# A list schedule's margin for matmuls fed by other engines, and seven edits beside it

## The chip, the cores and the metric

The kernel runs on one core of one Trainium2 chip. The metric is the device time of one execution in microseconds (us). Three runs of the kernel before took 1166.16, 1166.23 and 1167.39 us; the median is 1166.23 us. The trace is of one execution, taken by the hardware profiler.

## The reference

Two model blocks run one after the other on 256 tokens of 1024 features, in float32. The first block is two layers, each a mixer, a layer norm, a SwiGLU feed-forward part (2816 wide) and a second layer norm. The mixer of layer 0 joins stick-breaking attention and sparse attention over the 64 best keys of an indexer; that of layer 1 is differential attention. The second block puts 16 meta tokens ahead, and runs a gated linear recurrence (HGRN2) with short convolutions, an output product, a feed-forward part with a convolution, and RMS norms.

```python
def first_block(x, c, ...):
    mod = einsum('bd,ldm->lbm', silu(c), w_mod) + b_mod[:, None, :]
    for i in range(2):
        sh_m, sc_m, g_m, sh_f, sc_f, g_f = split(mod[i], 6)
        h = x * (1 + sc_m) + sh_m
        y = even_mixer(h, ...) if i % 2 == 0 else odd_mixer(h, ...)
        x = layer_norm(ALPHA * x + (1 + g_m) * y, ln_mix_g[i], ln_mix_b[i])
        h = x * (1 + sc_f) + sh_f
        y = (silu(h @ w_gate[i]) * (h @ w_up[i])) @ w_down[i]
        x = layer_norm(ALPHA * x + (1 + g_f) * y, ln_ffn_g[i], ln_ffn_b[i])

def hybrid_layer(h, lb, ...):                # second block, 16 meta tokens ahead
    q, f_raw, i_in, g_out, b_gate, c_gate, x_conv, gate_a, gate_b = split(rmsnorm(h) @ w_in)
    f = lb + (1 - lb) * sigmoid(f_raw)       # S_t = diag(f_t) S_{t-1} + (1 - f_t) v_t^T
    o = hgrn2(silu(q), 1 - f, i_in, log(f))  # o_t = S_t^T q_t
    ...
    h = h + merged @ w_out
    return h + (silu(conv(a)) * val) @ w_down   # a, val = rmsnorm(h) @ w_up
```

## The kernel before

Features lie on the partitions and the 256 tokens along the free dimension. Nearly all the work is products of activations with weights that stream from memory once, about 230 MB. A slab of weights (`stage`) is split by `fetch_half` into a high part `whi` (a copy on ScalarE) and a low part `wlo` (a subtraction on VectorE), and `mm3` multiplies the parts of weights and activations in three products per tile. The first slabs of the first product are used whole, as float32. The modulation vectors are a second stream: `mod_chunks` brings 96 chunks of 128x1024 through three buffers `mst`, and one VectorE operation multiplies and sums each.

A layer norm (`Norm`) takes its input by eight chunks `d0` to `d7` in `add`: a VectorE operation makes d from a product's bank, ScalarE squares it, and GpSimd adds the chunks into the sums `s1` and the squares into `s2`. At the last chunk, matmuls against a matrix of 1/1024 (`inv1024`) give mean and variance per token; `s1` and `s2` hold seven chunks and the eighth is a matmul operand of its own. Meanwhile the next product has started on the unnormalised operand `U`, which `scale_split` makes; these products are what TensorE can do while the statistics come. The five norms before the last are named here LN1 (after the output product of layer 0), LN2 (after its feed-forward part), LN3 and LN4 (the same in layer 1), and the RMS norm.

`gen_hgrn` runs twice, for four heads each. It first sums the log decays of the meta tokens backwards: 14 additions on GpSimd, each of which reads the one before. Then it builds a decay-weighted score matrix by levels `lv` of halved blocks: eight float32 matmuls of 128 by 128 columns into two banks, and a masked copy from each bank into `At`.

What runs when is not written out by hand. `Plan` records the operations of all engines, and `Plan.order` is a list schedule: it keeps an estimated time of each engine, and always issues the operation with the smallest due time among those that are ready. An operation becomes ready when the estimated end of what it needs, plus a gap, has come: `SELF` on one engine, `HOP` (300 ns) between two. `cost` gives the estimated duration by engine and size. Each engine then runs its list strictly in that order and waits on semaphores where something is late. Every instruction is issued from one helper, so in the profile all carry its line, L428 (L427 for ScalarE's table loads). Names in the profile are those of pools: `pa` is a PSUM bank, `w` a working tile, `sm` a small one, `cst` the constants.

Of the kernel before, what the change touches and what calls it, by code (L numbers as in the profile page):

```python
# [18 lines left out]
S = 256  # L19
# [7 lines left out]
EPS = 1e-6  # L27
# [42 lines left out]
class View:  # L70
    """A view of a planned tile; it becomes an access pattern once the tile has its buffer."""
# [33 lines left out]
class Plan:  # L105
    """Records engine operations in program order, orders them by a list schedule over estimated
    times that respects data dependences and buffer counts, and issues them in that order."""

    HOP = 300.0
    SETS = {AF.Exp: "natural_log_exp_and_others", AF.Ln: "natural_log_exp_and_others", AF.Silu: "silu_and_others",  # L110
# [67 lines left out]
    def cost(self, eng, op, writes, reads):  # L178
# [21 lines left out]
        if eng == "POOL":  # L200
            return 100.0 + n * 2.2
# [52 lines left out]
    def order(self):  # L254
# [177 lines left out]
def kernel(ctx, tc, io, out):  # L432
# [46 lines left out]
    class Vec8:  # L479
        """Feature chunks of up to 272 tokens, four to a tile."""  # L480
# [18 lines left out]
    def C(name, w=128):  # L499
        return cst[:, _C[name]:_C[name] + w]  # L500
# [66 lines left out]
    def add_plan(name, n, whole=0):  # L567
        """whole: so many slabs stay float32, and their products take float32's own passes"""
# [85 lines left out]
    def group(X, toks, ks=ALLK, outer=False):  # L654
        """one bank per column chunk; outer: the chunks advance together over k"""
# [8 lines left out]
    def gemm_pair(X):  # L664
        """both column chunks of a slab in one bank, 256 tokens"""
# [7 lines left out]
    def gemm_down(X, evac):  # L673
        """K = 2816"""
# [12 lines left out]
    def scale_split(Xh, Xl, src, g):  # L687
        """src * g in two parts, g per feature"""
# [6 lines left out]
    def root(dst, eps, src=None):  # L695
        """dst = 1 / sqrt(src + eps)"""
# [5 lines left out]
    class Norm:  # L702
        """t = ALPHA * x + (1 + g) * y by chunks, its mean and variance per token, and t * gain with
        (-gain, offset) columns as the moving operand of products that start before the statistics"""

        def __init__(self, xa, g1, lv, d=None, sq=None):
            self.xa, self.g1, self.lv, self.sq = xa, g1, lv, sq
# [8 lines left out]
        def add(self, k, y):  # L716
# [44 lines left out]
        def add_sq(self, k, d):  # L761
            """with LN = g * (t - mean) / std + b: the sums of (g t)^2, 2 g^2 t and 2 g b t"""
# [1079 lines left out]
```

## Time and profile before

| | |
|---|---|
| median of three runs | 1166.23 us |
| span of the profiled execution | 1163.9 us |
| mean granted TensorE clock | 0.989 of full speed |
| busy: TensorE, VectorE, ScalarE, GpSimd | 97%, 78%, 62%, 10% |
| read from memory | 229.8 MB, 198 GB/s over the span |

The span runs from the first to the last instruction of one execution; 2.3 us of the median run lie outside of it. PE is TensorE, DVE VectorE, ACT ScalarE, POOL GpSimd, SP the queue that issues the transfers. Since PE's ends are modelled, "97% busy" overstates it a little, and the small gaps are read from the wait rows and from the number of instructions in a stretch.

### The profile page before, as it was taken

Reading aid. Unit: us, or ns where it says so; the run is one execution under the profiler, and the core shown is the slowest. Engines: PE = TensorE matmul, PEld = TensorE weight load, DVE = VectorE, ACT = ScalarE, POOL = GpSimd, SP = SyncE. Lnnn points to the kernel's source line nnn. Section 1 sums busy time; section 2 is a strip of 40 time slices with the busy share of each in tenths; the row PEclk is TensorE's granted clock in tenths of the full one; section 3 lists DMA queues with packets and bytes.
Section 4 is the critical chain, followed back from the end, with each engine's and each line's share of the span. In section 5 each row is a group of like instructions: output and inputs, shape, how many; then the busy total and the mean of one; then the engine's idle time right before and its main releaser. Section 6 shows DMA issues by size and latency. Waiting matters only on the chain.

```text
span 1163.9 us, 22101 instructions
## 1 busy us (share of the span) xinstructions
PE 1125.9 (97%) x8769; PEld 1077.6 (93%) x8769; DVE 912.5 (78%) x1676; ACT 726.0 (62%) x1316; POOL 118.2 (10%) x127
## 2 busy tenths in 40 slices
PE   5999989999999999999999999999999999999997
PEld 4885889999999779899999999999999999999996
DVE  6799889988999999885558896896659978866642
ACT  3558657545448987664445567786758766655541
POOL 0110220000231302200003402000010011000011
PEclk9999989999999999899999999999999999999999
DMA  9938647998985425365544625244433325555441
GB/s 352 410 131 309 236 163 279 350 328 301 339 327 193 143 104 194 140 246 189 181 171 178 232 88 182 86 169 154 172 110 145 144 100 193 200 188 189 168 163 37
DMA packets 42248, 232.29 MB, mean 200 GB/s; under 512 B 4640, under 2 KB 6176, under 8 KB 24096
## 3 DMA queue, kind: packets, MB, share of 16 engines
q1 hardware_dynamic: 42144, 230.87, 54.4%
q8 instruction: 69, 1.13, 0.4%
q14 instruction: 35, 0.29, 0.1%
HBM read 229.81 MB, written 1.05 MB: 198 GB/s over the span
## 4 chain that ended last, share of the span: by engine, by line
PE 77%; DVE 11%; ACT 4%; DMA 4%; issue 2%; POOL 2%; DVEq 0%; SPq 0%; ACTq 0%; POOLq 0%
PE pa L428 77%; DVE w L428 5%; DVE wlo L428 3%; ACT w L428 2%; DMA mst<-in_wmod_dram 2%; POOL w L428 2%; DVE sm L428 2%; DVE mst L428 1%; ACT whi L428 1%; DMA whi<-in_w_dram 1%; DMA cst<-in_cst_dram 1%; ACT L427 0%; DMA vec<-in_vecs_dram 0%; ACT sm L428 0%; ACT scb L428 0%
## 5 line engine op out<-in xcount | busy, mean ns | idle before, releaser
L428 PE MATMUL pa<-w,whi 128*128 128x256 f32 (+4 forms) x5104 | 919.4, 288 | 8.5 <-DMA whi<-in_w_dram 7.6
L428 PEld LDWEIGHTS pa<-w,whi 128*128 128x128 f32 x5104 | 769.7, 190 | 16.9 <-ACT w L428 6.3
L428 PE MATMUL pa<-w,wlo 128*128 128x256 f32 (+3 forms) x2608 | 661.5, 289 | 0.0
L428 ACT ACTIVATE whi<-stage 128x1024 fp32r<-128x1024 f32 (+1 forms) x330 | 339.5, 1041 | 247.7 <-PE pa L428 217.8
L428 DVE TENSOR_TENSOR wlo<-stage,whi 128x1024 fp32r<-128x1024 f32 (+1 forms) x330 | 404.1, 1234 | 100.3 <-ACT whi L428 94.0
L428 PEld LDWEIGHTS pa<-w,wlo 128*128 128x128 f32 x2608 | 465.5, 190 | 7.0 <-issue 3.9
L428 ACT ACTIVATE w<-w 128x256 fp32r<-128x256 f32 (+9 forms) x257 | 117.3, 470 | 80.6 <-DVE w L428 66.9
L428 POOL TENSOR_TENSOR w<-w,w 128x256 f32<-128x256 f32 (+2 forms) x93 | 84.1, 917 | 521.6 <-ACT w L428 291.2
L428 ACT ACTIVATE w<-pa 128x256 f32<-128x256 f32 (+12 forms) x298 | 108.0, 392 | 46.0 <-PE pa L428 41.7
L428 DVE TENSOR_TENSOR w<-w,w 128x256 fp32r<-128x256 f32 (+7 forms) x263 | 121.5, 480 | 19.2 <-ACT w L428 15.7
L428 DVE SCALAR_TENSOR_TENSOR mst<-mst,scb 128x1024 f32<-128x1024 f32 x90 | 109.3, 1226 | 11.8 <-DMA mst<-in_wmod_dram 11.8
L428 DVE TENSOR_TENSOR w<-w,pa 128x256 f32<-128x256 f32 (+2 forms) x146 | 58.9, 418 | 60.9 <-PE pa L428 51.1
L427 ACT ACT_TABLE_LOAD x63 | 80.8, 1283 | 1.8 <-PEq L1832 0.7
L428 PE MATMUL pa<-w,w 128*128 128x128 f32 (+8 forms) x340 | 71.6, 336 | 1.2 <-DVE w L428 0.9
L428 PEld LDWEIGHTS pa<-w,w 128*128 128x128 f32 (+4 forms) x340 | 42.8, 176 | 10.6 <-issue 2.8
L428 PE MATMUL pa<-cst,w 128*128 128x128 f32 (+4 forms) x218 | 38.8, 268 | 12.6 <-POOL w L428 6.3
L428 PEld LDWEIGHTS pa<-cst,w 128*128 128x128 f32 (+2 forms) x218 | 27.8, 167 | 22.1 <-issue 7.5
L428 POOL TENSOR_TENSOR w<-w 128x256 f32<-128x256 f32 x4 | 3.2, 801 | 392.3 <-DVE w L428 392.3
L428 PE MATMUL pa<-w 128*128 128x128 f32 x240 | 35.0, 275 | 0.2 <-DVE w L428 0.2
L428 PE MATMUL pa<-whi,w 128*128 128x512 f32 x96 | 32.9, 417 | 0.0
L428 PEld LDWEIGHTS pa<-w 128*128 128x128 f32 x240 | 31.4, 191 | 0.4 <-issue 0.4
L428 POOL TENSOR_TENSOR w<-w,sinT 128x512 f32<-128x512 f32 (+1 forms) x14 | 20.4, 1454 | 107.0 <-ACT w L428 82.3
(145 smaller groups left out, 541.3 us busy)
## 6 DMA issues: line engine op xcount, KB each, us to landing
mst<-in_wmod_dram SPq DMA_DIRECT2D x90, 512.0 KB, 5.5
stage<-in_wgu_dram SPq DMA_DIRECT2D x44, 1024.0 KB, 5.0
stage<-in_wi_dram SPq DMA_DIRECT2D x36, 1024.0 KB, 4.8
stage<-in_wup_dram SPq DMA_DIRECT2D x22, 1024.0 KB, 4.8
stage<-in_wd_dram SPq DMA_DIRECT2D x24, 896.0 KB, 4.5
stage<-in_w_dram SPq DMA_DIRECT2D x15, 1024.0 KB, 7.1
stage<-in_wo_dram SPq DMA_DIRECT2D x12, 1024.0 KB, 4.8
stage<-in_wd_dram SPq DMA_DIRECT2D x12, 1024.0 KB, 4.8
```

The lines of the kernel that those rows point to most:

```text
L427: self.nc.scalar.preload_act_table_set(tables[i])
L428: fn(*[real(a) for a in args], **{k: real(a) for k, a in kw.items()})
```

## The change

Eight edits are made together.

- The schedule takes a TensorE operation as ready 1300 ns, not 300 ns, after the end of an operation on another engine that it needs (`SAFE`).
- The estimate for GpSimd rises from 100 + 2.2 n to 260 + 2.45 n ns.
- `inv1024` is no longer loaded but set on GpSimd. The first loads bring fewer columns of the constants and the vectors, the rest follows after the first product's loop, and the rotary tables are made at k = 5, not at k = 1.
- The mean of x is accumulated inside that loop, two chunks at a time, not behind it.
- LN2 and LN4 fold the eighth chunk into `s1` and `s2` with two VectorE additions; the statistics then take 4 matmuls, not 8.
- In both attentions of layer 0 the products with V, which fill 64 of the array's 128 columns, are written in pairs of the two halves.
- The decay sum of the meta tokens is done by doubling: four VectorE additions on 128 elements in place of 14 on GpSimd.
- At levels below 7 the decay matmuls move only the 64 columns that the mask keeps, into one bank, and one masked copy of half the size follows in place of two.

```diff
+    SAFE = 1000.0
...
         if eng == "POOL":
-            return 100.0 + n * 2.2
+            return 260.0 + n * 2.45
...
-                    at[j] = max(at[j], end + (self.SELF[e] if oj[0] == e else self.HOP))
+                    at[j] = max(at[j], end + (self.SELF[e] if oj[0] == e else self.HOP + self.SAFE if oj[0] == "PE"
+                                              else self.HOP))
...
-    run.sync.dma_start(vec, io["vecs"])
+    run.sync.dma_start(vec[:, :104], io["vecs"][:, :104])
     cst = const("cst", NCST)
-    run.sync.dma_start(cst[:, :128], io["cst"][:, :128])
+    run.sync.dma_start(cst[:, :130], io["cst"][:, :130])
+    inv1024 = const("inv1024", 128)
+    G.memset(inv1024, 1.0 / 1024)
...
             if k == 7:
                 sums = [(self.s1, d), (self.s2, sq)]
+                if self.fold:
+                    V.tensor_add(self.s1, self.s1, d)
+                    V.tensor_add(self.s2, self.s2, sq)
+                    sums = [(self.s1,), (self.s2,)]
...
-        if k == 1:
-            run.sync.dma_start(cst[:, 128:], io["cst"][:, 128:])
...
-        if k == 1:
+        if k % 2:
+            for kk in (k - 1, k):
+                T.matmul(ps_x, C("inv1024"), x0[kk // 4][:, kk % 4, :], start=kk == 0, stop=kk == 7)
+        if k == 5:
             rope_tables()
+    run.sync.dma_start(vec[:, 104:], io["vecs"][:, 104:])
+    run.sync.dma_start(cst[:, 130:], io["cst"][:, 130:])
...
-            for a in range(2):
-                for st in range(t + 1):
+            for st in range(t + 1):
+                for a in range(2):
                     T.matmul(ps[a * 64:a * 64 + 64, :].rearrange("p (j q) -> p j q", j=4), vtok[:, st, 0:64],
...
-        V.tensor_copy(su[:, 14, 0, :], lfm[:, :, 15])
-        V.memset(su[:, 14, 1, :], 0.0)
-        for s in range(13, -1, -1):
-            G.tensor_add(su[:, s], su[:, s + 1], lfm[:, None, :, s + 1].to_broadcast([128, 2, 4]))
+        su = su[:, 0:16]
...
+        for d in (1, 2, 4, 8):
+            V.tensor_add(sv[:, 0:16], su[:, 0:16], su[:, d:16 + d])
+            su, sv = sv, su
...
-                for hp in range(2):
-                    ps = bank("ps_h")
-                    for a in range(2):
-                        for t in range(2):
-                            xs = Xt[:, 2 * hp + a, t * 128:t * 128 + 128]
-                            T.matmul(ps[:, (a * 2 + t) * 128:(a * 2 + t) * 128 + 128], xs, xs, start=True, stop=True,
-                                     skip_group_check=True)
+                ps = bank("ps_h").rearrange("p (q i b) -> p q i b", q=8, b=B)
+                for h in range(4):
+                    for t in range(2):
+                        xs = Xt[:, h, t * 128:t * 128 + 128]
+                        T.matmul(ps[:, 2 * h + t], xs, xs.rearrange("p (i c b) -> p c i b", c=2, b=B)[:, 1], start=True,
+                                 stop=True, skip_group_check=True)
```

The order of every engine changes with the two edits of the schedule. The first place is VectorE ahead of LN1. Before, one modulation chunk (`mst`) stands between the norm's vectors (`lnv0lmg`) and d0 to d3 (`w_3_1286`, made from four banks):

```order
L428 TENSOR_TENSOR w_1_1270<-lnv0lmg_133,w_14_1266 128x4x2
L428 SCALAR_TENSOR_TENSOR mst_1216,raw_185<-mst_1216,scb_169 128x1024
L428 SCALAR_TENSOR_TENSOR w_3_1286<-pa_1099,mod_193,w_8_382 128x256
L428 SCALAR_TENSOR_TENSOR w_3_1286<-pa_1103,mod_193,w_8_382 128x256
L428 SCALAR_TENSOR_TENSOR w_3_1286<-pa_1120,mod_193,w_8_382 128x256
L428 SCALAR_TENSOR_TENSOR w_3_1286<-pa_1144,mod_193,w_8_382 128x256
L428 TENSOR_TENSOR wlo_1316<-stage_896,whi_1275 128x1024
```

Now four of these chunks stand there (one of them just ahead of the first row shown), and the low part of the last stick-breaking output (`w_18_1061`) between them:

```order
L430 TENSOR_TENSOR w_1_1265<-lnv0lmg_403,w_5_1261 128x4x2
L430 SCALAR_TENSOR_TENSOR mst_1208,raw_165<-mst_1208,scb_158 128x1024
L430 SCALAR_TENSOR_TENSOR mst_1233,raw_165<-mst_1233,scb_158 128x1024
L430 TENSOR_TENSOR w_18_1061<-pa_1273,w_4_1056 128x256
L430 SCALAR_TENSOR_TENSOR mst_1256,raw_165<-mst_1256,scb_158 128x1024
L430 SCALAR_TENSOR_TENSOR w_3_1320<-pa_1077,mod_173,w_8_355 128x256
L430 SCALAR_TENSOR_TENSOR w_3_1320<-pa_1096,mod_173,w_8_355 128x256
```

Three chunks have moved ahead of d0, and with it ahead of all that follows on VectorE.

The second place is VectorE at LN3, between d0 to d3 and d4 to d6 (`w_4_5431`). Before, two weight splits (`wlo`) and the operands U of all of d0 to d3 stand ahead of d4:

```order
L428 SCALAR_TENSOR_TENSOR w_18_5259<-w_15_5322,lnv1lmg_157,w_12_5254 128x256 x3
L428 TENSOR_TENSOR wlo_5393<-stage_5029,whi_5317 128x1024
L428 SCALAR_TENSOR_TENSOR w_18_5259<-w_15_5322,lnv1lmg_157,w_12_5254 128x256
L428 TENSOR_TENSOR wlo_5415<-stage_5188,whi_5386 128x1024
L428 SCALAR_TENSOR_TENSOR w_4_5431<-pa_5231,mod_193,w_3_3616 128x256
L428 SCALAR_TENSOR_TENSOR w_4_5431<-pa_5346,mod_193,w_3_3616 128x256
L428 SCALAR_TENSOR_TENSOR w_4_5431<-pa_5391,mod_193,w_3_3616 128x256
```

Now d4 (`w_4_5371`) stands ahead of both splits, and the others come one by one:

```order
L430 SCALAR_TENSOR_TENSOR w_18_5254<-w_0_5305,lnv1lmg_411,w_12_5250 128x256 x3
L430 SCALAR_TENSOR_TENSOR w_4_5371<-pa_5235,mod_173,w_3_3614 128x256
L430 TENSOR_TENSOR wlo_5379<-stage_5072,whi_5361 128x1024
L430 SCALAR_TENSOR_TENSOR w_18_5254<-w_0_5305,lnv1lmg_411,w_12_5250 128x256
L430 TENSOR_TENSOR wlo_5406<-stage_5121,whi_5382 128x1024
L430 SCALAR_TENSOR_TENSOR w_4_5371<-pa_5346,mod_173,w_3_3614 128x256
```

Here d4 has moved up by two weight splits and one U operation.

The third place is the decay sum of the meta tokens in the first half of `gen_hgrn`. Before, VectorE only prepares it (the copy and the memsets of `w_10_8450`), the 14 additions run on GpSimd, and VectorE takes their result for the decayed key `w_6_8515` behind three weight splits:

```order
L428 COPY w_10_8450<-w_2_8279 128x4
L428 MEMSET w_10_8450 128x4 x2
L428 TENSOR_TENSOR wlo_8456<-stage_8156,whi_8433 128x1024
L428 TENSOR_TENSOR wlo_8476<-stage_8314,whi_8447 128x1024
L428 MEMSET w_10_8450 128x4
L428 SCALAR_TENSOR_TENSOR w_4_8443<-w_7_8428,vec_98,w_4_8443 128x258 x2
L428 MEMSET w_6_8515 128x256
L428 MEMSET w_3_8521 32x128
L428 TENSOR_TENSOR wlo_8525<-stage_8314,whi_8466 128x1024
L428 TENSOR_TENSOR w_6_8515<-w_10_8450,w_2_8279 128x4x16 x2
```

Now all of it stands on VectorE, with the convolution's operations (`w_1_8450`, 258 columns) between; the decayed key is `w_10_8496`:

```order
L430 COPY w_7_8455<-w_2_8254 128x14x4
L430 TENSOR_TENSOR w_6_8463<-w_7_8455 128x128
L430 TENSOR_TENSOR w_7_8455<-w_6_8463 128x128
L430 SCALAR_TENSOR_TENSOR w_1_8450<-w_9_8426,vec_101,w_1_8450 128x258
L430 TENSOR_TENSOR w_6_8463<-w_7_8455 128x128
L430 TENSOR_TENSOR w_7_8455<-w_6_8463 128x128
L430 MEMSET w_7_8455 128x4
L430 SCALAR_TENSOR_TENSOR w_1_8450<-w_9_8426,vec_101,w_1_8450 128x258
L430 MEMSET w_10_8496 128x256
L430 TENSOR_TENSOR w_10_8496<-w_7_8455,w_2_8254 128x4x16 x2
```

The chain has moved from GpSimd to VectorE, and no weight split stands within it.

## Rows read from the trace of the kernel before

**Rows 1.** The page: busy time by engine, and the chain that ended last

```profile
PE 1125.9 (97%) x8769; PEld 1077.6 (93%) x8769; DVE 912.5 (78%) x1676; ACT 726.0 (62%) x1316; POOL 118.2 (10%) x127
PE 77%; DVE 11%; ACT 4%; DMA 4%; issue 2%; POOL 2%; DVEq 0%; SPq 0%; ACTq 0%; POOLq 0%
```

**Rows 2.** TensorE's waits: releaser, us in total, times, longest us

```profile
PE pa L428 <- DMA whi<-in_w_dram: 7.6, 3, 4.8
PE pa L428 <- DVE w L428: 6.4, 10, 2.1
PE pa L428 <- POOL w L428: 6.3, 4, 3.0
```

**Rows 3.** Stretches: length, then PE, PEld, DVE, ACT, POOL busy, PEclk, DMA, GB/s

```profile
200.00:220.00 20.00, 20.00 (x172) 20.00 (x171) 18.30 (x31) 12.94 (x18) 0.00 (x0) 1.00 0.93 346
155.00:161.80 6.80, 6.80 (x33) 6.80 (x34) 4.75 (x12) 2.11 (x3) 0.00 (x0) 0.50 0.74 265
472.40:479.30 6.90, 6.53 (x30) 6.54 (x31) 4.90 (x10) 1.82 (x3) 0.31 (x1) 0.51 0.49 161
721.60:728.40 6.80, 6.80 (x32) 6.54 (x32) 5.60 (x9) 5.00 (x7) 0.00 (x0) 0.50 0.44 154
```

**Rows 4.** Timeline of TensorE at the start: start, us, [idle before, releaser]

```profile
17.24 2.07 PE L428 MATMUL pa<-w,cst 128*128 128x256 f32 x4 [2.19 <-DMA cst<-in_cst_dram]
```

**Rows 5.** Timeline at LN1, all engines; last, transfers 130 to 145 us, issue to landing

```profile
153.20 0.38 PE L428 MATMUL pa<-cst,w 128*128 128x1 f32 x2 [2.98 <-POOL w L428]
137.66 1.66 DVE L428 SCALAR_TENSOR_TENSOR w<-pa,mod,w 128x256 f32<-128x256 f32 x4
149.96 0.47 DVE L428 SCALAR_TENSOR_TENSOR w<-pa,mod,w 128x256 f32<-128x256 f32 x1
158.67 1.22 DVE L428 SCALAR_TENSOR_TENSOR mst<-mst,scb 128x1024 f32<-128x1024 f32 x1
132.21 5.89 SPq L428 DMA_DIRECT2D mst<-in_wmod_dram  x4
mst<-in_wmod_dram SPq DMA_DIRECT2D x4, 512.0 KB, 4.5
```

**Rows 6.** The stretch of layer 1's attention, columns as in Rows 3

```profile
371.00:456.00 85.00, 80.69 (x522) 68.00 (x521) 82.52 (x195) 73.37 (x200) 15.36 (x11) 1.00 0.41 147
```

**Rows 7.** Timeline at LN3: TensorE, VectorE, GpSimd

```profile
471.10 1.05 PE L428 MATMUL pa<-cst,w 128*128 128x1 f32 x8 [2.08 <-POOL w L428]
461.71 1.76 DVE L428 TENSOR_TENSOR wlo<-stage,whi 128x1024 fp32r<-128x1024 f32 x1
465.41 1.25 DVE L428 SCALAR_TENSOR_TENSOR w<-pa,mod,w 128x256 f32<-128x256 f32 x3
466.02 6.69 POOL L428 TENSOR_TENSOR w<-w,w 128x256 f32<-128x256 f32 x6 [1.96 <-DVE w L428]
```

**Rows 8.** Timeline at the meta tokens: first half on four engines, second on GpSimd

```profile
711.95 6.86 POOL L428 TENSOR_TENSOR w<-w,w 128x8 f32<-128x8 f32 x14 [45.06 <-ACT whi L428]
718.84 0.31 ACT L428 ACTIVATE w<-w 128x128 f32<-128x128 f32 x1 [4.05 <-POOL w L428]
719.59 0.27 PE L428 MATMUL pa<-cst,w 128*32 128x128 f32 x1 [1.48 <-DVE w L428]
850.04 5.20 POOL L428 TENSOR_TENSOR w<-w,w 128x8 f32<-128x8 f32 x14 [131.24 <-DVE w L428]
```

**Rows 9.** TensorE's float32 matmuls, timeline: LN2's statistics, a decay level

```profile
346.83 1.62 PE L428 MATMUL pa<-cst,w 128*128 128x1 f32 x14
880.07 1.95 PE L428 MATMUL pa<-w 128*128 128x128 f32 x16
```

**Rows 10.** TensorE by form: xcount, busy us, mean ns, idle before

```profile
L428 PE MATMUL pa<-w,w 128*128 128x512 f32 x36 | 18.6, 598 | 0.0
L428 PE MATMUL pa<-w,w 128*64 128x512 f32 x12 | 4.1, 613 | 0.0
L428 PE MATMUL pa<-w,w 128*64 128x256 f32 x16 | 3.3, 404 | 0.0
L428 PE MATMUL pa<-w,w 128*64 128x128 f32 x16 | 2.1, 279 | 0.0
```

More of the change, by code (lines that the diff above doesn't have):

```diff
@@ L41 @@
 _n = 0
-for _name, _w in (("ident", 128), ("tn", 128), ("neg1", 128), ("inv1024", 128),
-                  ("causal", 128), ("strict", 128), ("inv", 1), ("sgn", 1)):
+for _name, _w in (("ident", 128), ("inv", 1), ("sgn", 1), ("tn", 128), ("neg1", 128),
+                  ("causal", 128), ("strict", 128)):
     _C[_name] = _n
@@ L499, in C @@
     def C(name, w=128):
-        return cst[:, _C[name]:_C[name] + w]
+        return inv1024[:, :w] if name == "inv1024" else cst[:, _C[name]:_C[name] + w]
     def VC(name, j, w=1):
@@ L702, with __init__ @@
     class Norm:
-        def __init__(self, xa, g1, lv, d=None, sq=None):
-            self.xa, self.g1, self.lv, self.sq = xa, g1, lv, sq
+        def __init__(self, xa, g1, lv, d=None, sq=None, fold=False):
+            self.xa, self.g1, self.lv, self.sq, self.fold = xa, g1, lv, sq, fold
             self.d = d or Vec8("d", S)
@@ L903 @@
     ws, pss = [], [gbank("ps_g") for _ in range((NST + 1) // 2)]
+    ps_x = bank("ps_s")[:, :S]
     for k in range(8):
@@ L921 @@
             split(X[0][k], X[1][k], Xf[k])
-    ps = bank("ps_s")
-    for k in range(8):
-        T.matmul(ps[:, :S], C("inv1024"), x0[k // 4][:, k % 4, :], start=k == 0, stop=k == 7)
     xm = w1("xm")[:, :S]
-    A.activation(xm, ps[:, :S], AF.Copy, scale=ALPHA)
+    A.activation(xm, ps_x, AF.Copy, scale=ALPHA)
     for k in range(8):
@@ L1135, in gen_sb @@
                          start=True, stop=False, skip_group_check=True)
+            for a in range(2):
+                h = 2 * j + a
                 T.matmul(ps[a * 64:a * 64 + 64, 128:256], vsb[:, 1, h * 64:h * 64 + 64],
@@ L1207 @@
     lv = ln_vectors(0, "lfg", "lfb", MV(1, 1, 0, 8), MV(1, 0, 0, 8))
-    norm = Norm(xa, MV(0, 5, 0, 8), lv)
+    norm = Norm(xa, MV(0, 5, 0, 8), lv, fold=True)
     gemm_down(Gp, norm.add)
@@ L1359 @@
     norm = Norm(xa, MV(1, 5, 0, 8), lnh, [H[k][:, NM:] for k in range(8)],
-                (lfg, lnh[:, 32:40], lnh[:, 40:48], lnh[:, 48:51]))
+                (lfg, lnh[:, 32:40], lnh[:, 40:48], lnh[:, 48:51]), fold=True)
     for i in range(2):
@@ L1439, in gen_hgrn @@
     def gen_hgrn(half, kt, km, q, P, lfm, vt, vm, qm):
-        su = w1("su")[:, :128].rearrange("p (s c h) -> p s c h", s=16, c=2)
-        V.memset(su[:, 15, 0, :], 0.0)
+        su, sv = [w1(n)[:, :192].rearrange("p (s c h) -> p s c h", s=24, c=2) for n in ("su", "sv")]
+        V.memset(su[:, 14:24], 0.0)
+        V.memset(sv[:, 16:24], 0.0)
+        V.tensor_copy(su[:, 0:15, 0, :], lfm[:, :, 1:16].rearrange("p h s -> p s h"))
+        V.tensor_copy(su[:, 0:14, 1, :], lfm[:, :, 1:15].rearrange("p h s -> p s h"))
+        for d in (1, 2, 4, 8):
+            V.tensor_add(sv[:, 0:16], su[:, 0:16], su[:, d:16 + d])
+            su, sv = sv, su
         V.memset(su[:, 15, 1, :], -1.0e4)
-        V.tensor_copy(su[:, 14, 0, :], lfm[:, :, 15])
-        V.memset(su[:, 14, 1, :], 0.0)
-        for s in range(13, -1, -1):
-            G.tensor_add(su[:, s], su[:, s + 1], lfm[:, None, :, s + 1].to_broadcast([128, 2, 4]))
+        su = su[:, 0:16]
         A.activation(su, su, AF.Exp)
@@ L1481, in gen_hgrn, with tiles @@
         V.memset(Sx, 0.0)
+        def tiles(t):
+            return t.rearrange("p a b -> p (a b)").rearrange("p (q n) -> p q n", n=128)
         def quads(t, hp):
@@ L1756, in lay_out @@
     cst[:, _C["neg1"]:_C["neg1"] + 128] = -1.0
-    cst[:, _C["inv1024"]:_C["inv1024"] + 128] = 1.0 / 1024
     cst[:, _C["causal"]:_C["causal"] + 128] = np.where(i[None, :] <= i[:, None], 0.0, NEG)
```

7 lines of the change are left out of this document (4 added, 3 removed).

## The prediction

> **What bounds the kernel now.** I read the page first. TensorE is busy for 1125.9 of 1163.9 us and makes up 77% of the chain that ended last, VectorE 11%, GpSimd 2% [rows 1]. So the kernel is bound by TensorE almost everywhere, and a change can win in three ways: less work on TensorE, a shorter wait of TensorE, or a better granted clock. The next view is the list of what TensorE waited for [rows 2]: transfers 7.6 us (all at the start), VectorE 6.4 in ten waits, GpSimd 6.3 in four. That is small, and it is all that a schedule can give back, apart from the clock. The third view is a table of stretches [rows 3]. At full clock 20 us hold 172 matmul records, 0.116 us each. In three stretches of 6.8 to 6.9 us the granted clock is at 0.50, the lower level of 1.2 GHz; they hold 30 to 33 records where 58 to 59 would fit, so each costs some 3 us. Each comes behind a place where TensorE stood still: 2.98 us at LN1 [rows 5], 2.08 us at LN3 [rows 7], 1.48 us at the meta tokens [rows 8]. Which of these waits goes, and whether its slow stretch goes with it, is the main question.
>
> **The start.** TensorE waits 2.19 us for the constants, and only for the rotary tables' transposes [rows 4]. The change moves both behind other work and takes some 0.4 MB (734 columns of 128 rows, and the 128 of `inv1024`) from ahead of the weights that are waited for, but one modulation chunk now comes earlier in the queue. Bounds 0 and 2.2; since the start is bound by transfers anyway, I take **-0.8**.
>
> **Products with V.** 64-column matmuls take 4.1 + 3.3 + 2.1 = 9.5 us [rows 10]. One of 512 columns takes 4.1/12 = 0.34 us a record where one over the whole array takes 18.6/36 = 0.52; so the two halves overlap in part already (0.66). If pairs overlapped wholly the ratio would be 0.5, and 9.5 x (1 - 0.5/0.66) = 2.3 us would go. Bounds 0 and 2.3; **-1.5**. The Trainium skill's page "TensorEngine Tiling (Array Packing)", section "Theoretical Speedup", allows up to twice the speed at 64 columns, which would be the same upper bound; the 0.66 shows that the written order now reaches it only in part.
>
> **LN1.** Here the change adds a wait. Three more modulation chunks stand on VectorE ahead of d0 to d3. In the trace they came far later, the first at 158.67 [rows 5]. The queue issues these transfers until 132.21 + 5.89 = 138.1 us, and one lands 4.5 us after its issue [rows 5], so the last of them lands at about 142.3, and its operation takes 1.22: d0 moves from 137.66 to about 143.5. (TensorE's order agrees in direction: the last products that d0 needs come some 40 products later.) From d0 to d6 VectorE took 149.96 - 137.66 = 12.3 us [rows 5]; with one U operation more d6 comes at about 156.5. Before, GpSimd was behind: the statistics waited until 153.20, 3.2 us after d6 began. Now d4 and d5 are summed early, and one addition of about 0.9 us (6.69/6 is 1.1 [rows 7]) follows d6: the first statistics matmul comes at about 158, 4.9 us later. TensorE has 9 more products to do before it (9 x 0.116 = 1.0). What is queued behind: the weight splits on VectorE, all 5 to 6 us later, hence TensorE's products on them. Bounds: -1 if the chunks land early enough for d0 to stay, +7 if the delay of d6 counts in full; **+3.5**. The slow stretch behind LN1 stays.
>
> **Folds at LN2 and LN4.** Eight matmuls fewer, two records each; LN2's took 1.62/14 = 0.116 us a record [rows 9]: 16 x 0.116 = 1.9 us. The four VectorE additions lie beside U's products; uncovered they would cost some 0.5 us each. Bounds -1.9 and 0; **-1.5**.
>
> **Layer 1's attention.** VectorE is busy for 82.5 of 85 us, TensorE shows 522 records and 80.7 us [rows 6]. By the order VectorE has some 2.4 us less to do there (two weight splits or chunks moved out). VectorE sets the pace here, so up to 2.4 us come back, less where TensorE waits for ScalarE (73.4 us busy); **-1.5**.
>
> **LN3.** GpSimd's second half waited 1.96 us for d4 [rows 7], which began at 465.41 behind two splits, the first at 461.71. Now d4 comes before both, so GpSimd can run through from the first half, some 2 us earlier, and d5, d6 follow one by one. TensorE's wait was 2.08. Bounds -2.7 (with the second wait there) and +0.5; **-2.0**.
>
> **Meta tokens.** 14 dependent additions on GpSimd take 6.86 us; ScalarE waits 4.05 us for them, TensorE 1.48 [rows 8]. The four doublings on VectorE are of 128 elements, and stand early enough to be done before TensorE asks; the second half has the same chain (5.20) with a wait of some 0.5. Next late is ScalarE's exponential, which is no longer held up. **-2.0**, bounds -2.5 and 0.
>
> **Decay levels.** 7 levels x 8 matmuls x 2 halves = 112 matmuls, 224 records. A record of 128 columns takes 1.95/16 = 0.122 us, one of a single column 1.62/14 = 0.116 [rows 9]. So columns hardly matter, and halving them gives at most 224 x 0.006/2 = 0.7; I take **0**. The smaller masked copies relieve VectorE where TensorE is the bound: 0. The Trainium skill speaks otherwise, in "TensorE: Matmul & The Clock Gate", section "Back-to-back issue gap": 134 cycles for 128 columns and about 60 for up to 64, which at 2.4 GHz would be 31 ns a record, 6.9 us in all. The row with one column speaks against it: whatever sets that record's time, it is not its columns.
>
> **The margin elsewhere.** A later ready time puts other products ahead of one that depends on another engine. What it saves is bounded by the remaining VectorE waits, some 3 us; what it can cost (a chain that goes back and forth moves on later) I bound by the same 3. **0**.
>
> **Clock.** One slow stretch of about 3 us goes, at LN3 or at the meta tokens, where the wait ahead of it goes: **-3.0**, bounds 0 and -6.
>
> **Sum.** -0.8 - 1.5 + 3.5 - 1.5 - 1.5 - 2.0 - 2.0 - 3.0 = -8.8. The span becomes 1155.1; with 2.3 us that lie around it in the median run, **1157.4 us**.
>
> **The rivals.** *Both slow stretches go and LN1 costs nothing:* 8.8 + 3 + 3.5 = 15.3 less, 1151 us. For it: the chunks' buffers may come free earlier; against it: 142.3 is read straight from the queue. *Hidden:* only fold, V and meta tokens count, LN1 costs its 3.5 and the clock stays: 1.5 + 1.5 + 2 - 3.5 = 1.5 less, 1164.7 us. For it: TensorE is 97% busy, and work freed on VectorE in layer 1 may only meet ScalarE. *Slower:* d0 waits for its three chunks, and all the splits behind it are late as well; TensorE runs dry inside the second group of the output product and again at d6 and d7: 7 us, and a longer standstill keeps the lower clock for a second stretch of 3 us. With only fold, V and meta tokens gained (5), that is 5 us more, 1171 us. It decides once LN1 costs over 7 us, which is when the last chunk lands after some 144 us. For it: VectorE is the engine that is late there. *Narrowing pays:* if half the columns took half the time, 224 x 0.122/2 = 13.7 us would go on top, 1144 us; with rows 9 against it, little chance.
>
> **How the numbers follow.** Forecast (own range 1153 to 1163.5) 0.47, both stretches 0.15, narrowing 0.04, hidden 0.16, slower 0.18. A measurement of this kernel tells 0.2%, 2.3 us, from no change. Faster: 0.47 + 0.15 + 0.04 = 0.66; same 0.16; slower 0.18. The range leaves out narrowing, the far part of the first rival and the far half of the slower one: 1149 to 1169.
>
> **What would show it.** Right: the wait for GpSimd at LN3 under 0.5 us; no wait ahead of the decayed key's transposes; at LN1 d0 near 143.5, with a wait of TensorE of 5 us or more in all; a record of 64 columns at a decay level as long as one of 128; at most two stretches at 0.50 after the start. Wrong: LN1 with no longer wait than 3 us, three slow stretches or none, or a lower mean time of a record at the decay levels. New waits in the list of TensorE's waits of over 3 us in total, on VectorE, would show that the margin costs.

## The result: 1.2% slower

The changed kernel took 1178.77 to 1187.27 us, median 1180.02, against 1166.2 for the kernel before: a ratio of 1.0118, 95% interval [1.0088, 1.0148]. The forecast was 1157.4, the range ended at 1169. The profiled execution has a span of 1176.8 us where it was 1163.9. The first rows of its page, and TensorE's waits (releaser, us in total, times, longest us), to be held against [rows 1, 2]:

```profile
span 1176.8 us, 22069 instructions
PE 1128.3 (96%) x8753; PEld 1077.6 (92%) x8753; DVE 912.1 (78%) x1676; ACT 718.1 (61%) x1309; POOL 108.4 (9%) x100
PE 76%; DVE 15%; ACT 4%; DMA 2%; issue 2%; SPq 0%; POOL 0%; DVEq 0%; ACTq 0%; POOLq 0%
```

```profile
PE pa L430 <- DVE w L430: 10.2, 11, 3.1
PE pa L430 <- DMA w<-in_xT_dram: 8.4, 2, 5.1
PE pa L430 <- ACT w L430: 6.6, 10, 1.4
PE pa L430 <- DVE wlo L430: 3.9, 6, 1.9
PE pa L430 <- DMA cst<-in_cst_dram: 3.4, 1, 3.4
PE pa L430 <- POOL w L430: 1.4, 2, 1.1
```

The work is the same and VectorE's share of the chain has grown from 11 to 15%. GpSimd, which held up TensorE for 6.3 us, now does so for 1.4; VectorE, with its weight splits, does so for 14.1 where it was 6.4.

**Where the time went.** Both kernels run the same 7856 products with streamed weights, nearly in the same order. So I took the start of the n-th of them in both traces and looked at how the lag grows from stage to stage. The stages are cut at products 420 (139 us of before), 700, 2080, 2300 (372 us), 2900, 4300, 4740, 4780 (731 us), 6000 (921 us) and 6100. Changes of the lag to the kernel before, in us, one profiled execution each:

| run | to LN1 | LN1 | LN2 | layer 1's attention, LN3 | LN4 to the meta tokens | meta tokens | decay levels | recurrence's end | all |
|---|---|---|---|---|---|---|---|---|---|
| the change | 2.9 | 5.1 | 6.3 | -1.7 | 2.4 | -6.0 | -0.7 | 5.3 | 12.6 |
| e1: no margin | 2.8 | -0.4 | -0.4 | 3.5 | -0.7 | -4.4 | 4.5 | -4.0 | 0.5 |
| e2: nor GpSimd estimate | 0.9 | 1.4 | -0.4 | 3.8 | 4.0 | -7.2 | 4.4 | -4.0 | 2.3 |
| e3: before, margin | 5.4 | 5.8 | 4.5 | -3.8 | 0.8 | -3.7 | -1.8 | 0.2 | 7.0 |
| e4: before, GpSimd estimate | 0.1 | 1.6 | 5.0 | -2.5 | 0.7 | -1.9 | 0.8 | 0.2 | 3.8 |
| e5: margin not at the norms | 2.9 | 8.1 | 4.4 | -3.1 | 3.9 | -6.0 | -0.7 | 8.2 | 17.0 |
| e6: nor in the recurrence | 2.3 | 8.1 | 4.4 | -1.5 | 2.3 | -7.3 | 4.3 | -4.6 | 7.9 |
| e7: no folds | 1.8 | 5.1 | 5.6 | -0.8 | 2.4 | -6.0 | -0.6 | 7.6 | 13.8 |
| e9: margin on products only | 4.8 | -3.5 | 6.1 | -5.2 | 5.0 | -7.2 | 4.3 | -4.0 | -0.4 |
| e10: on the small ones only | 5.8 | 3.0 | 1.6 | 1.1 | 1.0 | -4.8 | -0.6 | 8.8 | 14.3 |
| e8: before, decay sum and V | 0.8 | 0.1 | 0.0 | 0.0 | 0.2 | -3.1 | 0.5 | 0.0 | -1.4 |
| e11: e8 and levels | 2.4 | 0.2 | 0.0 | -0.6 | 2.8 | -4.4 | 4.2 | -4.0 | -0.6 |
| e12: e11 and folds | -0.3 | 0.1 | 6.6 | -1.6 | 1.3 | -2.9 | 5.8 | -4.0 | 3.8 |
| e13: margin of 300 ns | 1.2 | -2.1 | 7.6 | -6.2 | 1.7 | -2.9 | 3.8 | -4.6 | -1.4 |
| e14: e8, margin of -300 ns | 3.7 | 1.7 | 0.0 | 1.2 | 5.1 | -7.5 | -0.8 | 0.2 | 4.3 |

(The feed-forward stages and the end, where nothing moved by over 1.6 us, are left out of the columns but not of the sum. To the recurrence's levels and its end belong one another's gains and losses: a step that moves from one into the other shows in both.)

Three things have to be kept in mind with this table.

- An entry is one execution. e8 and e11 have the same order on TensorE up to some 700 us, as have e5 and e6, and their entries up to there still differ by up to 2.6 us. Executions of one kernel differ with the granted clock: e8's twelve take from 1159.58 us at a mean clock of 0.991 to 1166.06 us at 0.986. And e3's traced execution took 1172.82 us where its other three took 1178.58 to 1180.14.
- LN2 has to be read with the stage behind it. All nine runs that lose 4 us or more at LN2 gain in that stage, 0.8 to 6.2 us; in the change 6.3 - 1.7 = 4.6 us are left.
- The levels have to be read with the recurrence's end. There the change loses -0.7 + 5.3 = 4.6 us, e1 4.5 - 4.0 = 0.5.

The change loses at three places: 2.9 + 5.1 = 8.0 us up to the end of LN1, then at LN2 and at the recurrence's end.

**LN1** on VectorE and TensorE in the change (start, us, [idle before, releaser]); the last row is of the kernel before:

```profile
144.09 1.22 DVE L430 SCALAR_TENSOR_TENSOR mst<-mst,scb 128x1024 f32<-128x1024 f32 x1
146.07 1.66 DVE L430 SCALAR_TENSOR_TENSOR w<-pa,mod,w 128x256 f32<-128x256 f32 x4 [0.76 <-PE pa L430]
159.23 0.47 DVE L430 SCALAR_TENSOR_TENSOR w<-pa,mod,w 128x256 f32<-128x256 f32 x1
120.90 0.58 PE L430 MATMUL pa<-w,whi 128*128 128x256 f32 x1 [2.62 <-DVE w L430]
141.89 0.87 PE L430 MATMUL pa<-w,w 128*64 128x256 f32 x8
153.92 0.39 PE L430 MATMUL pa<-w,wlo 128*128 128x256 f32 x1 [1.90 <-DVE wlo L430]
161.47 0.38 PE L430 MATMUL pa<-inv,w 128*128 128x1 f32 x2 [1.12 <-POOL w L430]
177.43 0.47 PE L430 MATMUL pa<-w,whi 128*128 128x256 f32 x2 [0.87 <-DVE w L430]
133.63 0.88 PE L428 MATMUL pa<-w,w 128*64 128x256 f32 x8
```

Where [rows 5] had d0 at 137.66, it comes at 146.07, 8.4 us later. It stands behind the chunks, but they are not what delays it: VectorE waited for only one of them, 0.36 us, and at d0 it waits 0.76 us for TensorE's bank. Layer 0's last products with V, whose output the last products for d0 to d3 need, come 8.3 us later than before (141.89 and 133.63). In all sixteen kernels d0 follows the start of these eight by 3.1 to 5.0 us. The stage ahead already loses: at 120.90 a product waits 2.62 us for its operand (before, 0.28 us at 123.93). d6 comes at 159.23 (149.96 before), TensorE waits 1.90 us for a weight split, and the statistics start at 161.47 (153.20). Behind them are waits for h, the last of them 0.87 us, that the kernel before did not have.

**LN2** had no wait before. Now TensorE reaches the products on h before h is there:

```profile
368.62 0.38 PE L430 MATMUL pa<-w,whi 128*128 128x256 f32 x1 [0.22 <-DVE w L430]
369.90 0.58 PE L430 MATMUL pa<-w,whi 128*128 128x256 f32 x1 [0.78 <-ACT w L430]
371.15 0.77 PE L430 MATMUL pa<-w,whi 128*128 128x256 f32 x2 [0.67 <-DVE w L430]
```

The order tells why. Behind the broadcast transposes 61 products on U stood before, which took 7.3 us; in the change 26 stand there, and 38 instead of 27 between the last statistic and the transposes. The products that were to cover the chain from the transposes to h had been spent ahead of it. (In the runs below TensorE waits for h here by more than 0.3 us only where 26 or 30 products are left, in the change and in e10. The other losses at LN2 come with waits for weight splits, see the folds.)

**The recurrence's end** shows the same. The last decay level (128x128) stands behind all products that were left, 14.7 us after the level before it (6.7 us in the kernel before), and then nothing is left to cover the chain that follows: 1.36 + 0.69 + 3.06 us of waits.

```profile
921.97 1.90 PE L430 MATMUL pa<-w 128*128 128x64 f32 x16
936.69 1.16 PE L430 MATMUL pa<-w 128*128 128x128 f32 x8 [1.36 <-ACT w L430]
938.54 3.05 PE L430 MATMUL pa<-w,w 32*32 32x128 f32 x24 [0.69 <-ACT w L430]
944.64 0.51 PE L430 MATMUL pa<-w,whi 128*128 128x258 f32 x2 [3.06 <-DVE w L430]
```

**The clock.** Stretches as in [rows 3], six of the change at the lower level and one at the meta tokens:

```profile
14.90:25.20 10.30, 5.73 (x14) 4.53 (x15) 5.56 (x11) 1.09 (x2) 0.00 (x0) 0.50 1.03 408
120.70:124.10 3.40, 3.20 (x6) 1.99 (x7) 2.41 (x4) 0.03 (x1) 0.00 (x0) 0.50 0.70 248
154.90:158.30 3.40, 3.40 (x19) 3.40 (x18) 3.40 (x4) 1.39 (x2) 2.99 (x3) 0.50 0.82 296
178.80:182.20 3.40, 3.40 (x18) 3.40 (x17) 3.35 (x8) 3.37 (x7) 0.00 (x0) 0.50 0.02 5
369.90:376.70 6.80, 6.13 (x27) 5.86 (x28) 6.80 (x17) 6.65 (x13) 0.00 (x0) 0.50 0.00 0
486.00:492.80 6.80, 6.80 (x33) 6.80 (x33) 4.11 (x10) 3.27 (x4) 0.00 (x0) 0.50 0.71 252
723.00:730.00 7.00, 7.00 (x61) 7.00 (x60) 6.42 (x20) 5.85 (x11) 0.00 (x0) 1.00 0.40 150
```

At the meta tokens it stays at full speed, 61 records in 7 us where 32 were in 6.8. In exchange there is a slow stretch behind LN2's waits (27 records in 6.8 us, so some 31 fewer than fit, 3.6 us), and one of 3.4 us behind the wait at 120.90. Between the start, where TensorE waits for transfers, and the last 10 us the kernel before has 20.5 us in three stretches at the lower level, the change 23.8 us in five. So in sum the clock gave nothing back: its mean is 0.982 where it was 0.989.

### The profile page after: what moved, and what is told of

It is laid out like the page before. It is cut to its first block, busy times and chain, and to the rows that moved or that the text cites. A ratio compares the mean times of both kernels' runs of the same rounds, so it can differ in the third digit from the quotient of the medians.

```text
span 1176.8 us, 22069 instructions
## 1 busy us (share of the span) xinstructions
PE 1128.3 (96%) x8753; PEld 1077.6 (92%) x8753; DVE 912.1 (78%) x1676; ACT 718.1 (61%) x1309; POOL 108.4 (9%) x100
## 4 chain that ended last, share of the span: by engine, by line
PE 76%; DVE 15%; ACT 4%; DMA 2%; issue 2%; SPq 0%; POOL 0%; DVEq 0%; ACTq 0%; POOLq 0%
PE pa L430 76%; DVE w L430 8%; DVE wlo L430 4%; ACT w L430 3%; DVE sm L430 2%; DMA w<-in_xT_dram 1%; DVE mst L430 1%; ACT whi L430 1%; DMA mst<-in_wmod_dram 0%; DVE lbt L430 0%; SPq L430 0%; POOL w L430 0%; ACT L429 0%; DVE lnh L430 0%; DVEq L1855 0%
## 5 line engine op out<-in xcount | busy, mean ns | idle before, releaser
L430 ACT ACTIVATE w<-w 128x256 fp32r<-128x256 f32 (+8 forms) x257 | 116.9, 468 | 78.7 <-DVE w L430 66.0
L430 DVE TENSOR_TENSOR w<-w,w 128x256 fp32r<-128x256 f32 (+6 forms) x267 | 123.7, 482 | 10.0 <-ACT w L430 7.9
L430 POOL TENSOR_TENSOR w<-w,w 128x256 f32<-128x256 f32 (+1 forms) x65 | 75.4, 1182 | 528.0 <-ACT w L430 477.7
L430 PE MATMUL pa<-w,w 128*128 128x128 f32 (+8 forms) x340 | 65.5, 330 | 3.5 <-DVE w L430 1.2
L430 PEld LDWEIGHTS pa<-w,w 128*128 128x128 f32 (+4 forms) x340 | 39.9, 172 | 12.3 <-ACT w L430 3.4
L430 PE MATMUL pa<-w 128*128 128x64 f32 (+1 forms) x240 | 29.5, 270 | 1.4 <-ACT w L430 1.4
L430 PEld LDWEIGHTS pa<-w 128*128 128x128 f32 x240 | 28.8, 191 | 1.6 <-ACT w L430 1.6
L430 DVE SCALAR_TENSOR_TENSOR w<-pa,vec,w 128x256 f32<-128x256 f32 (+1 forms) x48 | 23.1, 481 | 5.7 <-PE pa L430 5.0
L430 PE MATMUL pa<-cst,w 128*128 128x128 f32 (+2 forms) x122 | 25.2, 274 | 2.2 <-DVE sm L430 1.2
```

Of the source, the lines that this page charges most:

```text
L430: fn(*[real(a) for a in args], **{k: real(a) for k, a in kw.items()})
```

## The experiments

Ratios are to the kernel before on the same chip.

**The margin alone.** e1 sets it to 0 in the change; e2 takes the GpSimd estimate back as well; e3 and e4 put the one or the other into the kernel before.

```diff
-    SAFE = 1000.0
+    SAFE = 0.0        # e1, e2
-            return 260.0 + n * 2.45
+            return 100.0 + n * 2.2    # e2
```

> The changed kernel with the margin SAFE set to 0, all else kept. Theory M (the margin): it makes the schedule put products on U ahead of the statistics' transposes (38 between the last statistic and the transposes at LN2 where 27 stood), so only 26 products on U are left behind them (61 before) and TensorE runs dry; here 46 stand behind them at LN2 and 56 at LN1. M expects the losses at LN1 (6.9 us), behind LN2 (5 to 7) and at the end of the second half of the recurrence (5.7) to go, and the gains at the meta tokens (5.9) to stay: 1156 to 1163 us. Theory E (the other edits moved the order, the margin is innocent): 1176 to 1182 us. Theory S (any edit scatters the list schedule by some us either way): anywhere from 1160 to 1180 with new losses at other places.

> The changed kernel without the margin and with the old GpSimd estimate: only the six code edits. M: 1156 to 1164, within 3 us of the run without the margin alone. E: 1176 to 1182. A theory that the GpSimd estimate does the harm at LN1 (it also sets where VectorE's modulation chunks stand ahead of d0) expects the difference between this and the run without the margin alone to be over 4 us.

> The kernel before with the margin of 1000 ns alone. M: the same loss as in the change without its gains at the meta tokens: 40 to 44 products on U are left behind the transposes at LN1 to LN3 (59, 61, 57 before), so TensorE waits for h behind LN1 and LN2 and the recurrence's end comes late: 1172 to 1185 us. E: within 3 us of before, 1163 to 1169.

> The kernel before with the higher GpSimd estimate alone. M: within 3 us of before, since 53 to 60 products on U stay behind the transposes: 1163 to 1169. The theory that the GpSimd estimate does the harm at LN1: 1170 to 1175.

Measured: e1 0.9999 [0.9980, 1.0017], 1166.95 us; e2 1.0012 [0.9995, 1.0029], 1168.53 us; e3 1.0098 [1.0062, 1.0133], 1178.97 us; e4 1.0028 [1.0010, 1.0045], 1169.8 us. The margin costs what the whole change costs, on either base: theory E falls. Theory S, that any edit scatters the schedule, does not fall by e1, whose time lies in its range. But of all runs of this section, the five kernels with 1000 ns on the small operations of attention and recurrence (the change, e3, e5, e7, e10) lie 0.9 to 1.2% above the kernel before, e6, which frees the recurrence, 0.6%, and the nine others between -0.5 and 0.3%. M was too hopeful of the rest (1156 to 1163 us for e1): without the margin the losses at LN1, LN2 and the recurrence's end are gone and the meta tokens' gain is there, yet other stages (layer 1's attention 3.5, up to LN1 2.8) give it back. And the GpSimd estimate is not quite innocent: 5.0 us at LN2. In e3 d0 at LN1 comes even later, and TensorE waits 2.65 us for GpSimd. At the recurrence's end, where M expected a loss, e3 has none: the last level stands 8.1 us behind the one before it, and no wait follows. The narrowed levels without the margin (e11) have none either, so the loss there needs the margin together with another of the edits; which one was not tried.

```profile
149.92 1.66 DVE L430 SCALAR_TENSOR_TENSOR w<-pa,mod,w 128x256 f32<-128x256 f32 x4
165.46 0.38 PE L430 MATMUL pa<-cst,w 128*128 128x1 f32 x2 [2.65 <-POOL w L430]
929.90 1.06 PE L430 MATMUL pa<-w 128*128 128x128 f32 x8
```

**Which operations' margin.** TensorE's operations have banks by their use, so the margin can be left off by bank. e5 leaves it off at the norms' statistics and transposes, e6 in the recurrence too; e9 keeps it on products with streamed weights only, e10 on all but these.

```diff
-self.HOP + self.SAFE if oj[0] == "PE"
+self.HOP + (0.0 if any(x[:4] in ("ps_s", "ps_b") for x in oj[6]) else self.SAFE) if oj[0] == "PE"          # e5
+self.HOP + (0.0 if any(x[:4] in ("ps_s", "ps_b", "ps_h") for x in oj[6]) else self.SAFE) if oj[0] == "PE"  # e6
+self.HOP + (self.SAFE if any(x[:4] in ("ps_g", "ps_d", "ps_v") for x in oj[6]) else 0.0) if oj[0] == "PE"  # e9
+self.HOP + (0.0 if any(x[:4] in ("ps_g", "ps_d", "ps_v") for x in oj[6]) else self.SAFE) if oj[0] == "PE"  # e10
```

> The changed kernel with the margin kept everywhere but at the norms' statistics and broadcast transposes (those with a bank of the statistics or of the broadcast). M, as it stands now: at each norm the margin moved these few operations behind products on U, which are then missing behind them. 40 products stand behind the transposes at LN2 here (26 in the change, 61 before), 49 at LN1 (39, 59). So the 6 us lost behind LN2 go, and some 2 to 3 of the 7 at LN1; the loss at the end of the recurrence (6) stays: 1169 to 1174 us. If LN's order is not the reason: 1178 to 1182.

> As the run with the norms freed of the margin, and free of it also in the recurrence's decay sums and scores (operations with a bank of that part). M: the last level stood 14.7 us behind the level before it since the margin put all remaining products ahead of it, and 5 us of waits followed; that goes too: 1162 to 1168 us. If the recurrence's end comes late for another reason (fewer steps per level since the levels were narrowed): as the run with the norms freed alone, within 2 us.

> The changed kernel with the margin only on products with streamed weights (operations with a bank of the products), none on the small operations of attention, norms and recurrence. Theory M2: the harm comes from chains that go back and forth between TensorE and other engines (statistics, attention, decay levels), where each TensorE step is put later; the products themselves have their operands long before. 44 to 61 products on U stay behind the transposes. So the losses behind LN2 and at the recurrence's end go and most of the one at LN1: 1164 to 1170 us. Theory M3: it is the products' own margin (on weight splits and on outputs of the attention) that makes d0 at LN1 late and lets the splits run dry behind LN2: 1173 to 1181.

> The opposite: the margin only on the small operations, none on the products with streamed weights. Only 28, 30 and 39 products on U stay behind the transposes at LN1 to LN3 (59, 61, 57 before). M2: the full loss, 1176 to 1184 us, with the last decay level 12 us or more behind the one before it. M3: 1164 to 1171.

Measured: e5 1.0106 [1.0074, 1.0138], 1180.58 us, a miss; e6 1.0056 [1.0035, 1.0078], 1174.35 us, a miss too; e9 0.9998 [0.9979, 1.0016], 1166.56 us; e10 1.0092 [1.0057, 1.0126], 1178.11 us. In total the pair e9 and e10 settles M2 against M3: the margin on the products is free, that on the small operations is the whole loss. (M2 also expected LN2's loss to go in e9, and it did not: 6.1 us, of which the stage behind it gives back 5.2.) e6 against e5 shows the recurrence: levels and end together go from 7.5 to -0.3 us, as the last level comes 6.3 us behind the one before it; in e10 it is 14.7 again, with the wait of 3.05. First e6, then e10:

```profile
918.96 1.89 PE L430 MATMUL pa<-w 128*128 128x64 f32 x16
925.22 1.05 PE L430 MATMUL pa<-w 128*128 128x128 f32 x8
```

```profile
920.52 1.89 PE L430 MATMUL pa<-w 128*128 128x64 f32 x16
935.22 1.16 PE L430 MATMUL pa<-w 128*128 128x128 f32 x8 [1.36 <-ACT w L430]
943.17 0.76 PE L430 MATMUL pa<-w,whi 128*128 128x258 f32 x2 [3.05 <-DVE w L430]
```

What fell is my reading of LN1: freeing the statistics and transposes (e5) made it worse, 8.1 us. Ahead of LN1, e6 and e9 differ only in the small operations of layer 0's attention with its indexer, and in a few transposes at the start. The last products with V begin at 141.30 us in e6 and at 138.66 in e9, and the loss up to the end of LN1 goes from 10.4 us to 1.3; e6 spends 17.1 us up to there at the lower clock, e9 6.8. So LN1's loss comes from the margin inside layer 0's attention, whose outputs the last products ahead of d0 need, and not from the statistics.

**The folds.** e7 takes them out of the change; e12, below, puts them into a kernel without margin.

```diff
-    norm = Norm(xa, MV(0, 5, 0, 8), lv, fold=True)
+    norm = Norm(xa, MV(0, 5, 0, 8), lv)
-                (lfg, lnh[:, 32:40], lnh[:, 40:48], lnh[:, 48:51]), fold=True)
+                (lfg, lnh[:, 32:40], lnh[:, 40:48], lnh[:, 48:51]))
```

> The changed kernel without the folds at LN2 and LN4. The loss behind LN2 appears with the change (6 us) but hardly with the margin alone on the kernel before (1 us), so the fold is a partner in it: two more VectorE additions ahead of the statistics, and 26 products left behind the transposes. Here 40 are left. M: 4 to 5 us of the 6 go, less 1.9 for the eight matmuls that come back: 1175 to 1179 us. If the fold is innocent: 1180 to 1183.

Measured: 1.0108 [1.0078, 1.0138], 1180.97 us, no difference to the change. The waits behind LN2 were then others (for weight splits), and the loss there was 5.6 us instead of 6.3.

**Edits without the schedule's.** e8 is the kernel before with the decay sum by doubling and the paired products with V; e11 adds the narrowed levels, e12 the folds. The edits' code is that of the change.

> The kernel before with two edits alone, the decay sum by doubling on VectorE and the paired products with V; neither moves the norms in TensorE's order (59, 61, 57 products on U behind the transposes, as before). Products with V: 64-column matmuls took 9.5 us before and 7.2 in the change, so 1 to 2.3 us. Decay sum: the change gained 6 us over that stretch, the change without the margin 4.4; 3 to 6 us with the slow stretch behind it gone, 1.5 if that stays. Together 1158 to 1163 us, and faster than both kernels. If the gains at the meta tokens came from the margin or from the whole reshuffle: 1164 to 1167.

> The kernel before with the whole edit of the recurrence (decay sum by doubling and narrowed levels with one masked copy) and the paired products with V; the order up to the recurrence is that of the run with decay sum and pairs alone (1163.0 us). Narrowing takes no time off a matmul (0.112 us a record at 64 columns as at 128), but there is one masked copy and one step fewer at each level; the change without the margin gained 5.2 us from the meta tokens to the RMS norm, the run with the decay sum alone 2.6. If that difference is due to the levels: 1159 to 1161.5 us. If it was the order: 1162 to 1165.

> As the run with the recurrence and the pairs, with the folds at LN2 and LN4 added. The folds take eight matmuls, 1.9 us, off TensorE but leave 46 products on U behind LN2's transposes (61 without). If those still cover the chain: 1 to 2 us faster than without the folds. If not (the first VectorE additions come ahead of the statistics, and the order behind moves): the same or up to 4 us slower.

Measured: e8 0.9954 [0.9936, 0.9973], 1163.01 us; e11 0.9964 [0.9942, 0.9986], 1164.51 us; e12 1.0025 [1.0010, 1.0041], 1169.86 us. e8 beats both kernels, on its two edits alone: the transposes at the meta tokens have no wait any more (1.48 us in [rows 8]),

```profile
719.63 0.27 PE L428 MATMUL pa<-cst,w 128*32 128x128 f32 x1
```

and its slow stretch there lasts 3.4 us, not 6.8 (another of 3.4 us comes at 855.8 us). The levels add nothing that can be measured. The folds cost 5 us on this base, at LN2 (6.6, with a slow stretch of 6.8 us in it): only 46 products on U are left there, and behind them ScalarE has its operations on h, one weight copy, and four operations of another kind ahead of the other copies, so the splits come late. TensorE and ScalarE of e12:

```profile
366.68 0.58 PE L428 MATMUL pa<-w,wlo 128*128 128x256 f32 x1 [1.18 <-DVE wlo L428]
368.65 0.79 PE L428 MATMUL pa<-w,whi 128*128 128x256 f32 x2 [0.33 <-ACT whi L428]
```

```profile
364.97 2.54 ACT L428 ACTIVATE w<-w 32x512 f32<-32x512 f32 x4
367.54 3.90 ACT L428 ACTIVATE whi<-stage 128x1024 fp32r<-128x1024 f32 x4
```

In e1, with the same 46 products left, one weight copy stands among the operations on h and two more ahead of the four others, and LN2 loses nothing. This holds over all kernels with 40 or more products left at LN2. With three copies in time (the kernel before, e1, e2, e8, e11, e14; 46 to 64 products) nothing is lost; with two (e3, e5, e6, e7; 40 products) or one (e4, e9, e12, e13; 44 to 60) 4.4 to 7.6 us are, with waits for the splits. The change and e10 have three copies, and there the longest wait is for h. So LN2 tips by what stands ahead of the splits on ScalarE, and the number of products decides only where it is small.

**How much margin.** e13 is the change with 300 ns, e14 is e8 with -300 ns, where no gap is left between the engines.

> The changed kernel with a margin of 300 ns in place of 1000. 38, 44 and 44 products on U stay behind the transposes at LN1 to LN3 (39, 26, 44 in the change; 56, 46, 58 without a margin). If the loss goes with what is left behind the transposes, most of LN1's and half of LN2's stay: 1170 to 1176 us. If it goes with the margin's size: 1169 to 1171. If only a margin beyond what the hand-over really takes does harm: 1166 to 1168.

> The kernel before with the decay sum by doubling and the paired products with V, and a margin of -300 ns: TensorE's operations count as ready without any gap. 69, 64 and 64 products on U stay behind the transposes (59, 61, 57 before). If an earlier place of the statistics keeps paying, it is 2 to 4 us faster than the two edits alone (1163.0): 1159 to 1161. If TensorE then meets operands that are not there yet, at each of the small operations: 1164 to 1172, with more waits for VectorE and ScalarE than the two edits alone have.

Measured: e13 0.9969 [0.9944, 0.9993], 1164.18 us; e14 1.0003 [0.9982, 1.0024], 1168.96 us. e13 is faster than each of its three expectations; e14 is slower than e8 with an interval that does not meet e8's. So the loss does not grow evenly with the margin, nor with the number of products left behind the transposes: e13 has 38, 44 and 44 and no loss at LN1. It begins somewhere between 300 and 1000 ns, and a gap too short costs as well. At LN1 d0 follows the margin: 140.61 us without it (e1), 141.58 in e13, 146.07 in the change. First e1, then e13:

```profile
140.61 1.65 DVE L430 SCALAR_TENSOR_TENSOR w<-pa,mod,w 128x256 f32<-128x256 f32 x4
141.58 1.66 DVE L430 SCALAR_TENSOR_TENSOR w<-pa,mod,w 128x256 f32<-128x256 f32 x4 [0.16 <-PE pa L430]
```

## Why the prediction was wrong

- **The margin elsewhere: 0, bounds 3 either way.** This step failed. I bounded the margin's cost by the waits that were there to be saved. A cost has no such bound: what the margin spends are the independent products that cover a chain, and there were 7 us of them behind each norm. It costs about 11 us alone (e3), all of it on small operations within chains (e9, e10). Against e1 the change loses 5.6 us up to the end of LN1 (8.0 and 2.4), 4.1 over the levels and the recurrence's end (4.6 and 0.5), and 1.5 at LN2 with the stage behind it (4.6 and 3.1). With the margin alone only the first of these shows (e3: 11.2, -1.6 and 0.7). I had the number of products on U in the order and read them only ahead of the statistics, not behind the transposes. The sign that I had named for a costly margin came: TensorE's waits for VectorE grew by 7.7 us.
- **LN1: +3.5, bounds -1 and +7.** Direction right, too small (5.1, and 8.0 with the stage ahead of it), and not by the mechanism that I gave. I let d0 wait for the last chunk; VectorE waited only 0.36 us for one of the chunks, and d0 came at 146.07 where I put 143.5, since the last products with V were 8.3 us late. (My sum was off by 0.3 as well: 138.1 + 4.5 is 142.6.) d6 at 159.23 (156.5), the statistics at 161.47 (158). The waits for h behind it were not foreseen. The slower rival had this place and a price of 7, and it lacked the other two places.
- **Folds: -1.5.** No gain: in the change, taking them out alters nothing (e7), and without the margin they cost 5 us (e12). Eight matmuls less were worth 1.9 us at most; two more VectorE additions ahead of the statistics, which I called covered, change the order behind them: 46 products left at LN2 where there were 61, and one weight copy in time where there were three.
- **Start: -0.8.** No gain: the lag is 0.4 us at the first product, 0.5 at the 200th. I misread [rows 4]: the rotary tables have no operation on TensorE, and the matmuls that waited for the constants there are the mean of x, for `inv1024`. That wait went, and the mean of x inside the loop now stands in TensorE's queue ahead of other products and waits for x:

```profile
8.65 2.05 PE L430 MATMUL pa<-w,inv 128*128 128x256 f32 x4 [3.34 <-DMA w<-in_xT_dram]
19.47 2.08 PE L430 MATMUL pa<-w,inv 128*128 128x256 f32 x4 [5.09 <-DMA w<-in_xT_dram]
```

- **Products with V: -1.5.** 3.0 + 2.6 + 1.6 = 7.2 us where [rows 10] had 9.5: the upper bound of 2.3 was right, in TensorE's own work. But the pairing in the code is not what it hangs on: e3 and e4, without it, take 7.2 us too, and e8, with it, 8.2. The order that the schedule makes decides which halves meet. The gain lies in the stage up to LN1, which lost 2.9 in all.

```profile
L430 PE MATMUL pa<-w,w 128*64 128x512 f32 x12 | 3.0, 601 | 0.0
L430 PE MATMUL pa<-w,w 128*64 128x256 f32 x16 | 2.6, 398 | 1.1 <-DVE lnv0lmg L430 1.1
L430 PE MATMUL pa<-w,w 128*64 128x128 f32 x16 | 1.6, 273 | 0.0
```

- **LN3 and meta tokens: -2.0 each, and one slow stretch, -3.0.** Right at these places, but not for the clock in sum: two other slow stretches came (120.7 and 369.9 us), where I had put none. GpSimd runs through at LN3 without the pause of [rows 7], TensorE's wait for it fell from 2.08 to 0.24, and the lag falls by 2.2 between products 2700 and 2800. At the meta tokens the wait and the slow stretch went, 6.0 us against the 5.0 that I had. GpSimd and TensorE at LN3, then TensorE at the meta tokens:

```profile
471.49 13.75 POOL L430 TENSOR_TENSOR w<-w,w 128x256 f32<-128x256 f32 x11
483.62 0.38 PE L430 MATMUL pa<-inv,w 128*128 128x1 f32 x2 [0.24 <-POOL w L430]
731.01 0.27 PE L430 MATMUL pa<-cst,w 128*32 128x128 f32 x1
```

- **Decay levels: 0.** Right. Sixteen records of 64 columns take 1.89 us where sixteen of 128 took 1.95 [rows 9]; the rule of halved time for 64 columns that the Trainium skill gives ("TensorE: Matmul & The Clock Gate", "Back-to-back issue gap") does not hold for these float32 matmuls.

```profile
876.16 1.89 PE L430 MATMUL pa<-w 128*128 128x64 f32 x16
```

- **Layer 1's attention: -1.5.** Not seen: together with LN3 this stage gained 1.7, which LN3 explains. In e1 and e2, without the margin, it even lost 3.5 to 3.8.

What stays open: why the loss sets in between 300 and 1000 ns and not evenly, and how the stage of layer 1's attention gives back what LN2 loses. Which single operation of layer 0's attention delays the last products with V, and which edit the margin needs beside it to hurt at the recurrence's end, was not tried.

## What to carry to other kernels

A safety margin in a schedule's estimates does not only make an engine wait less: it moves independent work from behind a dependent step to ahead of it, and a chain that comes back to the engine needs that work a second time. Before such an edit, count for each chain what independent work stands behind its last hand-over, not only ahead of its first, and compare its time with the chain's. The count is not all: at LN2 the order of ScalarE's weight copies decided in most runs. Put a margin, if any, on operations that end a chain (the large products here) and not on those within one; and measure code edits apart from the schedule's, since two of these eight, alone, made the kernel 0.5% faster, and all eight together 1.2% slower.

## What was unexpected of the hardware

TensorE's lower clock level came for 3.4 us as well as for 6.8: 19 records in 154.9 to 158.3 us, 27 in 369.9 to 376.7. Two products with V that stand next to each other, each on half of the array's columns, overlap fully: 0.25 us a record at 512 columns (3.0/12), half of the 0.52 over the whole array [rows 10].
